# Both halves merged together: branch and output weights loaded once, the output projection by row tiles, the second norm's sums on ScalarE

## The chip, the cores and the metric

The kernel runs on one core of a Trainium2 chip. The metric is the device time of one execution in microseconds (us), here the median of three runs; 0.2% of it is 3.1 us. The engines are TensorE (PE: matmuls and transposes), VectorE (DVE), ScalarE (ACT), GpSimd (POOL) and SyncE (SP, which here only issues transfers). Each runs its own list of instructions in order; a row at the head of a list that waits holds up all behind it. Operands lie in SBUF (128 partitions), matmul results in PSUM.

## The reference, cut to what matters

```python
# S = D = 1024, one sequence, one layer
proj = h @ w_in                       # q, k, v of two attention branches, two gates
o_a  = forgetting_attention(...)      # (S, 512): rows 0..3 of o in tiles of 128
o_c  = chunk_band_attention(...)      # (S, 512): rows 4..7 of o
merged = sigmoid(gate_a) * (o_a @ w_br_fox) + sigmoid(gate_c) * (o_c @ w_br_chunk)
mix  = merged @ w_out
x    = layer_norm(alpha * x + (1 + g1) * mix, ln1_g, ln1_b)
h    = layer_norm(x) * (1 + sc2) + sh2
u    = causal_depthwise_conv(h @ w_up, conv_w, conv_b)
...                                   # silu(a) * val, @ w_down, third norm
```

The change concerns the lines from `merged` to `h`.

## The kernel before, in words

All matmuls are float32 products made of three passes: each operand is split into a high and a low part (`hi`, and `lo = x - hi`), and the product is hi·hi + lo·hi + hi·lo (`mm3`, L192 to L194, and three matmuls in `add`, L954 to L956). One matmul takes a 128x128 block against 512 columns. The sequence is worked on in two halves of 512 tokens. Tiles stand transposed (channels on partitions) up to the merge.

The stage runs between the last gate products (psg) and the main up-projection. For each half:

- `load_o` brings o in four pairs of tiles (4, 6, 2, 0; 4 to 7 belong to the second branch): raw o from DRAM (`ost`, 512 KB), the softmax factors r broadcast over rows (`ort`, two transfers of 256 KB), their product on VectorE (L793), the high part on ScalarE (`oh`, L796), the low part on VectorE (`ol`, L797).
- `merge` makes, for each of eight column tiles c, two branch products (psb; branch 1 then branch 0, four k tiles each, 12 matmuls a branch) from the branch weights `brd[c]` (two transfers of 512 KB, high and low), multiplies each with its gate (`sgl`, read from `gd`, L928), adds the two (L934) and splits the sum (`mh` on ScalarE L937, `ml` on VectorE L938).
- `mix` is the output projection: eight k tiles of weights `wod[k]` (two transfers each) against four row tiles, two column halves (psm). Half 0 goes through k on the outside and four row tiles inside; half 1 takes k = 0 so, and the other k row tile by row tile, with more buffers for the weights (`wide`). Then per row tile the residual (L981, L982).
- `norms` makes two layer norms per row tile: the first with gain and bias (L991, L992), stored to `xd`; the second without (`normalise`: sums by bn_stats L119, final scaling on ScalarE L140). For half 0 it is stepped inside merge(1), one step per c, so VectorE has it between the gate products.
- `turned_0` and `turned_1` transpose the second norm's result (L1004), scale it by the modulation (L1006) and split it into operands: half 0's `ha`, `hb` and half 1's differences `hc`.

Then come eight heads (`head`, psu, L859), each 24 matmuls, whose weights are split by `ready` (L847, L848); turned_1 is stepped between them, its first step ahead of all heads that follow the first two.

The order of each engine's list is set by the framework's scheduler from the order in which the program is written and from its own estimates; the buffers of a pool (`bufs`) decide when a transfer may be issued. All transfers of weights, gates, o and x in this stage are issued by SP, one list. Half 1's o is read during mix(0), one pair per k from the third on:

```python
reading = load_o(1, o1, (4, 6, 2, 0), mx, "xr", 4, mx, "xr")
xs0 = mix(0, m0, chain((None,) * 2, reading))
beside = norms(0, xs0, x0)
m1 = merge(1, o1, beside, ahead)
```

Of the kernel before, what the change touches and what calls it, by code (L numbers as in the profile page):

```python
# [19 lines left out]
P = 128  # L20
# [24 lines left out]
def body(ctx, tc, a, out):  # L45
# [735 lines left out]
    sy.dma_start(out=g1row, in_=rowd[0].partition_broadcast(P))  # L781
    o_cm, op_ = opened(name="o", bufs=1, side="right")

    def load_o(half, os_, pairs, pool, tag, bufs, rpool, rtag, early=0):
        for n, i in enumerate(pairs):
# [3 lines left out]
            rt = rpool.tile([P, 2, H], F32, name=nm("ort"), tag=rtag, bufs=4)  # L789
# [13 lines left out]
    reading = load_o(0, o0, (4, 6, 2, 0), ap0, "qs", 4, ap0, "m1", 3)  # L803
# [13 lines left out]
    h_11, h_21 = operands(hap, "ha"), operands(hap, "hb")  # L817
# [3 lines left out]
    mx_cm, mx = opened(name="mx", bufs=2)  # L821
# [46 lines left out]
    def ready(c, pool=None, raws_in=None):  # L868
# [8 lines left out]
        st = raws_in.tile([P, 2, H], F32, name=nm("sgl"), tag="sgl", bufs=2).rearrange("p j (k n) -> p (j k) n", k=4)  # L877
# [24 lines left out]
    if True:  # L902
# [11 lines left out]
        def merge(half, os_, beside, ahead=iter(())):  # L914
            ms = []
            held = {}

            def branch(c, b):
                if c not in held:
                    sg = mx.tile([P, 2, H], F32, name=nm("sgl"), tag="sgl", bufs=2)  # L920
                    sy.dma_start(out=sg, in_=gd[half, 2 * c : 2 * c + 2].rearrange("b p s -> p b s"))
                    held[c] = [x.rearrange("p j (k n) -> p (j k) n", k=4) for x in parted_w(brd[c])], sg
                (bh, bl), sg = held[c]
                ps = mxp.tile([P, H], F32, name=nm("psb"), tag="mm")
                for k in range(4):
                    kk = 4 * b + k
                    mm3(ps, bh[:, kk, :], bl[:, kk, :], os_[kk][0], os_[kk][1], k == 0, k == 3)
                ve.scalar_tensor_tensor(out=sg[:, b, :], in0=sg[:, b, :], scalar=1.0, in1=ps, op0=ALU.add, op1=ALU.mult)  # L928

            for c in range(KD):  # L930
                branch(c, 1)
                branch(c, 0)
                sg = held.pop(c)[1]
                ve.tensor_tensor(out=sg[:, 0, :], in0=sg[:, 0, :], in1=sg[:, 1, :], op=ALU.add)  # L934
                mh = mx.tile([P, H], F32R, name=nm("mh"), tag=f"mh{c}", bufs=1)
                ml = mx.tile([P, H], F32R, name=nm("ml"), tag=f"ml{c}", bufs=1)
                se.copy(out=mh, in_=sg[:, 0, :])  # L937
                ve.tensor_sub(out=ml, in0=sg[:, 0, :], in1=mh)  # L938
                ms.append((mh, ml))
                next(ahead, None)  # L940
                next(beside, None)
            return ms

        def mix(half, ms, beside, wide=None, ended=None, rest=None):
            ps = [
                [(mxt if t == 3 else mxp).tile([P, H], F32, name=nm("psm"), tag="tt" if t == 3 else "mm") for _ in range(2)]
                for t in range(4)
            ]

            def add(t, k, w):  # L950
                mh, ml = ms[k]
                ts = slice(t * P, (t + 1) * P)
                for n in range(2):
                    pe.matmul(ps[t][n], mh[:, ts], w[0][:, n, :], start=k == 0, stop=False)  # L954
                    pe.matmul(ps[t][n], mh[:, ts], w[1][:, n, :], start=False, stop=False)
                    pe.matmul(ps[t][n], ml[:, ts], w[0][:, n, :], start=False, stop=k == end)  # L956

            end = 3 if wide else KD - 1
            late = []
            for k in range(1 if wide else KD):  # L960
                w = parted_w(wod[k])
                for t in range(4):
                    add(t, k, w)
                next(beside, None)
            if wide:
                late += [(k, parted_w(wod[k])) for k in (1, 2)]
                late += sorted(wide.items()) + [(k, parted_w(wod[k], rest)) for k in (6, 7)]
# [6 lines left out]
            if wide:  # L974
                late.append((3, parted_w(wod[3])))
# [484 lines left out]
```

## Time and profile before

| | |
|---|---|
| timed, median of three | 1547.22 us (1544.13 to 1547.38) |
| span of the profiled execution | 1548.2 us |
| TensorE busy | 1502.7 us, 97% |
| VectorE / ScalarE busy | 1034.5 us, 67% / 709.5 us, 46% |
| chain that ended last | PE 72%, POOL 9%, DMA 8%, DVE 7% |
| transfers | 317.54 MB, mean 205 GB/s |

The profile is of one execution, its time 1.0 us over the median of the timed ones. Times on its axis are us from the start of the span. A matmul's record overlaps the next one's: 0.39 us is from start to end, and what counts in a row of matmuls is the distance of their starts. "Granted clock" (PEclk) is TensorE's clock as a share of 2.4 GHz; it has the two levels 1.00 and .50 (1.2 GHz), and a window that holds both shows a value between. A wait in the profile names what ended it. "Idle before" on an engine that nobody waits for costs nothing.

### The profile page before, as it was taken

The page shows a single profiled execution, that of the slowest core. Times are in us where ns is not written, and L with a number is a line of the kernel's source. Part 1 is how long each engine was busy: PE and PEld are TensorE (multiplying, and loading weights), DVE is VectorE, ACT ScalarE, POOL GpSimd, SP SyncE. Part 2 cuts the span into 40 slices and gives each one's busy share as a digit, 9 for nine tenths or more (in the row PEclk, how much of TensorE's full clock was granted, in tenths as well). Part 3 has the DMA queues.
Part 4 walks back from the last instruction along what each step waited for, and adds up shares of the span by engine and source line. Part 5 has one row for each costly group of instructions (what it writes and reads, how often), then busy time and mean ns, then how long its engine had stood idle before and what let it go on. Part 6 is the DMA issues. An engine that isn't in the chain of part 4 may idle for free.

```text
span 1548.2 us, 21760 instructions
## 1 busy us (share of the span) xinstructions
PE 1502.7 (97%) x7663; PEld 1264.7 (82%) x7663; DVE 1034.5 (67%) x2038; ACT 709.5 (46%) x1316; POOL 658.2 (43%) x607
## 2 busy tenths in 40 slices
PE   6999999999999999999998999999999999999996
PEld 3788898889889888888886877888888888888885
DVE  6756566566656565554468587777778776845798
ACT  3545555554544454442112165544544554555451
POOL 0039897787878776730000005454455443000000
PEclk9999999999999999999999999999999999999998
DMA  9156666756576578758999575443344322697552
GB/s 366 50 165 215 217 192 198 218 194 216 189 233 220 189 260 299 260 151 292 308 323 347 214 258 190 140 154 132 122 140 147 115 102 104 246 328 255 191 190 75
DMA packets 129756, 317.54 MB, mean 205 GB/s; under 512 B 13024, under 2 KB 21936, under 8 KB 129648
## 3 DMA queue, kind: packets, MB, share of 16 engines
q1 hardware_dynamic: 90208, 197.83, 37.8%
q0 software_dynamic: 25344, 92.02, 17.8%
q10 hardware_dynamic: 14096, 26.31, 4.8%
q8 instruction: 60, 0.98, 0.3%
q14 instruction: 48, 0.39, 0.1%
HBM read 223.47 MB, written 84.25 MB: 199 GB/s over the span
## 4 chain that ended last, share of the span: by engine, by line
PE 72%; POOL 9%; DMA 8%; DVE 7%; issue 2%; ACT 1%; SPq 0%; ACTq 0%; DVEq 0%; POOLq 0%
PE psu L859 25%; PE psd L1277 4%; PE psd L1278 4%; PE psd L1276 4%; PE pso L508 3%; DMA wod<-dr 3%; PE psg L192 3%; PE psg L194 3%; PE psg L193 3%; POOL dr L553 2%; PE pst L494 2%; POOL acc L559 2%; POOL dr L556 2%; PE psq L194 2%; DMA brd<-dr 2%
## 5 line engine op out<-in xcount | busy, mean ns | idle before, releaser
L859 PE MATMUL psu<-hc,wx 128*128 128x512 f32 x792 | 185.7, 389 | 0.1
L859 PEld LDWEIGHTS psu<-hc,wx 128*128 128x128 f32 x792 | 148.6, 188 | 31.3 <-ACT u L1202 0.5
L1125 DVE SCALAR_TENSOR_TENSOR pcv<-u,convp,pcv 128x1024 f32<-128x1024 f32 x88 | 113.1, 1286 | 45.4 <-ACT pcv L1123 44.4
L1266 DVE TENSOR_TENSOR op<-rw,op 128x512 fp32r<-128x512 f32 x146 | 93.4, 687 | 52.8 <-ACT op L1265 52.5
L1265 ACT CAST op<-rw 128x512 fp32r<-128x512 f32 x146 | 85.2, 622 | 85.4 <-PE psd L1278 39.8
L457 ACT ACTIVATE s<-s,mx 128x640 f32<-128x640 f32 (+7 forms) x128 | 94.5, 738 | 58.6 <-DVE mx L451 57.4
L1277 PE MATMUL psd<-op,op 128*128 128x512 f32 x292 | 113.6, 389 | 0.9 <-DVE op L1266 0.9
L1278 PE MATMUL psd<-op,op 128*128 128x512 f32 x292 | 113.6, 389 | 0.0
L1276 PE MATMUL psd<-op,op 128*128 128x512 f32 x292 | 113.1, 389 | 0.0
L497 ACT CAST pt<-pst 128x512 fp32r<-128x512 f32 (+1 forms) x192 | 82.1, 450 | 62.3 <-PE pst L494 60.8
L498 DVE TENSOR_TENSOR pt<-pst,pt 128x512 fp32r<-128x512 f32 (+1 forms) x192 | 96.0, 519 | 17.2 <-ACT pt L497 15.5
L192 PE MATMUL psq<-h1h,wh 128*128 128x512 f32 x256 | 103.8, 407 | 1.7 <-DVE h1h L188 1.3
L192 PE MATMUL psg<-h1h,wh 128*128 128x512 f32 x256 | 103.7, 405 | 0.0
L194 PE MATMUL psq<-h1h,wl 128*128 128x512 f32 x256 | 100.9, 394 | 0.9 <-DVE wl L112 0.9
L194 PE MATMUL psg<-h1h,wl 128*128 128x512 f32 x256 | 100.3, 392 | 0.5 <-DVE wl L112 0.5
L193 PE MATMUL psq<-h1l,wh 128*128 128x512 f32 x256 | 100.8, 394 | 0.0
L193 PE MATMUL psg<-h1l,wh 128*128 128x512 f32 x256 | 100.2, 391 | 0.0
L556 POOL TENSOR_SCALAR dr<-dr,cond 128x512 f32<-128x512 f32 x56 | 89.9, 1607 | 8.1 <-DMA dr<-in_w_ada 7.1
L508 PE MATMUL pso<-pt,vs 128*128 128x256 f32 x608 | 90.4, 288 | 1.3 <-DVE pt L498 1.2
L994 POOL DMA_DIRECT2D xd<-xr x8 | 4.4, 545 | 199.3 <-DVE xr L992 199.3
L508 PEld LDWEIGHTS pso<-pt,vs 128*128 128x128 f32 x608 | 81.1, 191 | 8.7 <-DVE pt L498 2.6
L112 DVE TENSOR_TENSOR wl<-ws,wh 128x1024 fp32r<-128x1024 f32 x38 | 61.2, 1611 | 39.1 <-ACT wh L111 39.1
(286 smaller groups left out, 4001.3 us busy)
## 6 DMA issues: line engine op xcount, KB each, us to landing
ws<-in_w_up SPq DMA_DIRECT2D x34, 512.0 KB, 3.7
dr<-in_w_ada POOLq DMA_DIRECT2D x32, 512.0 KB, 4.8
dr<-in_w_down POOLq DMA_DIRECT2D x22, 512.0 KB, 4.8
td<-dr POOLq DMA_DIRECT2D x22, 512.0 KB, 4.7
rw<-td SPq DMA_DIRECT2D x44, 256.0 KB, 4.5
yd<-y SPq DMA_DIRECT2D x20, 512.0 KB, 2.7
rw<-yd SPq DMA_DIRECT2D x40, 256.0 KB, 4.2
rw<-sd SPq DMA_DIRECT2D x33, 256.0 KB, 4.6
```

The costliest lines, as they stand in the source:

```text
L192: pe.matmul(ps, wh, xh, start=start, stop=False)
L193: pe.matmul(ps, wh, xl, start=False, stop=False)
L194: pe.matmul(ps, wl, xh, start=False, stop=stop)
L457: se.activation(out=st[:, 0:nk], in_=st[:, 0:nk], func=AF.Exp, scale=-1.0, bias=prev, accum_out=sums[:, col : col + 1])
L498: ve.tensor_sub(out=dl, in0=src, in1=dh)
L508: pe.matmul(ps[:, 0:256], vs[:, h % 2, j0 + j, :], pt[j // 4][:, c, j % 4, :], start=j == 0 and c == 0, stop=j == nj - 1 and c == 1)
L556: po.tensor_scalar_mul(x[:, k % 2, :] if k else acc, x[:, k % 2, :], cond[:, k : k + 1])
L859: pe.matmul(ps, w[:, a_, k, :], h[k][b_], start=first, stop=k == 3 and a_ == 1, skip_group_check=on)
L1125: ve.scalar_tensor_tensor(out=ps, in0=u[b][:, 2 - d : S + 2 - d], scalar=cp[:, 2 - d : 3 - d], in1=ps, op0=ALU.mult, op1=ALU.add)
L1276: pe.matmul(ps[t], g[:, 0, ts], d[:, 0], start=start, stop=False, skip_group_check=on)
L1277: pe.matmul(ps[t], g[:, 0, ts], d[:, 1], start=False, stop=False, skip_group_check=on)
L1278: pe.matmul(ps[t], g[:, 1, ts], d[:, 0], start=False, stop=stop, skip_group_check=on)
```

## The change

- Both halves are merged in one pass: for c = 0 and 1 all of half 0's units come first, then half 1's; for c from 2 on each c is done for half 0 and half 1. Half 1's o is read during the first four units, through two staging buffers that later hold output weights. Each `brd[c]` is loaded once.
- The merged tiles of both halves stay in SBUF, and so do all eight `wod[k]`, loaded once.
- The output projection goes by row tiles over the whole sequence: tiles 0 and 1 together, then 2 to 7 one at a time, each over all k. Residual and norms of a tile follow it.
- For tiles 0 to 6 the second norm's sum and sum of squares are made by ScalarE (Identity and Square with an accumulated output, L989 and L994 of the new kernel), its root by `rooted`; tile 7 keeps `normalise`.
- Half 0's transposes are stepped after the row tiles 5 and 6, through the transposes' own PSUM buffers; half 1's first step comes after the third head in place of before it.

```diff
-    def load_o(half, os_, pairs, pool, tag, bufs, rpool, rtag, early=0):
+    def load_o(half, os_, pairs, pool, tag, bufs, rpool, rtag, op_, early=0):
...
-            rt = rpool.tile([P, 2, H], F32, name=nm("ort"), tag=rtag, bufs=4)
+            rt = rpool.tile([P, 2, H], F32, name=nm("ort"), tag=rtag, bufs=bufs)
...
+            order_ = [(0, 1, 0), (0, 0, 0), (1, 1, 0), (1, 0, 0), (0, 1, 1), (1, 1, 1), (0, 0, 1), (1, 0, 1)]
+            order_ += [(c, b, half) for c in range(2, KD) for half in range(2) for b in (1, 0)]
+            for n, unit in enumerate(order_):
+                branch(*unit)
+                if n < 4:
+                    next(reading)
...
+        def norms(t, xx, x2, on_act):
...
+            se.activation(out=x2, in_=xx, func=AF.Identity, accum_out=s1)
+            yield
+            ve.tensor_scalar_mul(nmean, s1, -1.0 / D)
+            se.activation(out=x2, in_=xx, func=AF.Square, bias=nmean, accum_out=s2)
+            yield
+            ve.tensor_scalar(out=v, in0=s2, scalar1=1.0 / D, scalar2=EPS, op0=ALU.mult, op1=ALU.add)
+            r = rooted(v)
+            ve.tensor_tensor(out=b, in0=nmean, in1=r, op=ALU.mult)
+            se.activation(out=x2, in_=xx, func=AF.Identity, scale=r, bias=b)
...
-        m0 = merge(0, o0, iter(()))
-        reading = load_o(1, o1, (4, 6, 2, 0), mx, "xr", 4, mx, "xr")
-        xs0 = mix(0, m0, chain((None,) * 2, reading))
-        beside = norms(0, xs0, x0)
-        m1 = merge(1, o1, beside, ahead)
-        turning = turned_0(x0)
-        xs1 = mix(1, m1, iter(()), wide, turning, hdp)
+        ms = merge((o0, o1), load_o(1, o1, (4, 6, 2, 0), wop, "wh", 2, wop, "wl", o1p))
+        ws = [parted_w(wod[k], wop) for k in range(2)] + [parted_w(wod[k]) for k in range(2, 5)]
+        ws += [parted_w(wod[k], w2p) for k in range(5, KD)]
+        for group in ((0, 1), (2,), (3,), (4,), (5,), (6,), (7,)):
+            rows(min(NT, group[-1] + 3))
+            for k in range(KD):
+                for i, t in enumerate(group):
+                    mixed(t, ws, ms, ps[i], k)
+            if turning:
+                for _ in range(2):
+                    next(turning, None)
+            for i, t in enumerate(group):
+                residual(ps[i], xs[t])
+            for t in group:
+                begin(t)
+            if group == (4,):
+                turning = turned_0(x2s)
+            if group == (6,):
+                for c in range(EARLY):
+                    ready(c, hdp, mx)
...
-    next(turns)
     for c in range(EARLY, HEAD):
         head(c)
         next(turns, None)
```

TensorE at the start of the merge, before: from half 0's c = 1 (weights wh_7958) to its c = 2 (ws_7997, loaded ahead); oh and ol are tiles of half 0's o.

```order
L194 MATMUL psb_7976<-oh_7810,wl_7959 128x512
L192 MATMUL psb_8001<-oh_7790,ws_7997 128x512
L193 MATMUL psb_8001<-ol_7791,ws_7997 128x512
L194 MATMUL psb_8001<-oh_7790,ws_7998 128x512
...
L192 MATMUL psb_8001<-oh_7800,ws_7997 128x512
...
L192 MATMUL psb_8015<-oh_7876,ws_7997 128x512
L193 MATMUL psb_8015<-ol_7877,ws_7997 128x512
```

TensorE at the same place after the change: oh_7936 is half 1's pair 4, oh_7965 pair 6, oh_8024 pair 0, oh_7995 pair 2; ws_8098 is c = 2.

```order
L194 MATMUL psb_7999<-oh_7813,wl_7970 128x512
L192 MATMUL psb_8030<-oh_7936,wh_7910 128x512
L192 MATMUL psb_8046<-oh_7936,wh_7969 128x512
...
L192 MATMUL psb_8030<-oh_7965,wh_7910 128x512
L192 MATMUL psb_8046<-oh_7965,wh_7969 128x512
...
L192 MATMUL psb_8060<-oh_8024,wh_7910 128x512
L192 MATMUL psb_8079<-oh_8024,wh_7969 128x512
...
L192 MATMUL psb_8060<-oh_7995,wh_7910 128x512
...
L192 MATMUL psb_8104<-oh_7793,ws_8098 128x512
```

After 48 matmuls of half 0 come half 1's units of c = 0 and 1 in the order of pairs 4, 6, 0, 2; c = 2 of half 0, which followed at once before, stands behind all of them.

SP's list at the same place, before: wh_7958 and wl_7959 are the weights of c = 1, ost_8323 the first pair of half 1's o.

```order
L911 DMA wh_7958<-brd 128x2x512
L911 DMA wl_7959<-brd 128x2x512
L921 DMA sgl_7917<-gd 128x2x512
L921 DMA sgl_7956<-gd 128x2x512
L911 DMA wh_8036<-brd 128x2x512
L911 DMA wl_8037<-brd 128x2x512
L788 DMA ost_8323<-od 128x2x512
L921 DMA sgl_7995<-gd 128x2x512
```

SP's list after: the four pairs of half 1 are ost_7930, ost_7959, ost_7989 and ost_8018; sgl are gates.

```order
L913 DMA wl_7970<-brd 128x2x512
L926 DMA sgl_7914<-gd 128x2x512
L789 DMA ost_7930<-od 128x2x512
L793 DMA ort_7932<-rd 64x2x512 x2
L789 DMA ost_7959<-od 128x2x512
L793 DMA ort_7961<-rd 64x2x512 x2
L926 DMA sgl_7973<-gd 128x2x512
L789 DMA ost_7989<-od 128x2x512
...
L789 DMA ost_8018<-od 128x2x512
...
L926 DMA sgl_8044<-gd 128x2x512
```

Behind c = 1's weights the o loads of half 1 have moved up, ahead of the gates and weights of the later c; the third and fourth pair use the staging buffers of the first and second.

VectorE at that place after the change: L794 is the product with r, L798 the low part of o, L932 the gate product, L935 and L941 sum and split of a merged tile.

```order
L794 TENSOR_TENSOR ost_7930<-ost_7930,ort_7932 128x1024
L798 TENSOR_TENSOR ol_7937<-ost_7930,oh_7936 128x1024
L794 TENSOR_TENSOR ost_7959<-ost_7959,ort_7961 128x1024
L932 SCALAR_TENSOR_TENSOR sgl_7973<-sgl_7973,psb_7975 128x512
L932 SCALAR_TENSOR_TENSOR sgl_7973<-sgl_7973,psb_7999 128x512
L798 TENSOR_TENSOR ol_7966<-ost_7959,oh_7965 128x1024
L935 TENSOR_TENSOR sgl_7973<-sgl_7973 128x512
L941 TENSOR_TENSOR m_8015<-sgl_7973,m_8014 128x512
L794 TENSOR_TENSOR ost_7989<-ost_7989,ort_7991 128x1024
...
L794 TENSOR_TENSOR ost_8018<-ost_8018,ort_8020 128x1024
```

Before, no work on half 1's o stood here:

```order
L797 TENSOR_TENSOR ol_7877<-ost_7870,oh_7876 128x1024
L928 SCALAR_TENSOR_TENSOR sgl_7917<-sgl_7917,psb_7923 128x512
L928 SCALAR_TENSOR_TENSOR sgl_7917<-sgl_7917,psb_7937 128x512
L934 TENSOR_TENSOR sgl_7917<-sgl_7917 128x512
L928 SCALAR_TENSOR_TENSOR sgl_7956<-sgl_7956,psb_7962 128x512
L938 TENSOR_TENSOR ml_7953<-sgl_7917,mh_7952 128x512
L928 SCALAR_TENSOR_TENSOR sgl_7956<-sgl_7956,psb_7976 128x512
...
L928 SCALAR_TENSOR_TENSOR sgl_7995<-sgl_7995,psb_8001 128x512
```

The low part of the second pair (ol_7966) now stands behind two gate products (sgl_7973), and the fourth pair's product behind that.

VectorE in the second merge before: L119, L121, L123 and L127 to L139 are half 0's second norm; L928, L934 and L938 are the merge.

```order
L938 TENSOR_TENSOR ml_8859<-sgl_8823,mh_8858 128x512
...
L119 BN_STATS st_8867<-xr_8505 128x6
...
L928 SCALAR_TENSOR_TENSOR sgl_8886<-sgl_8886,psb_8892 128x512
L121 BN_AGGR mv_8870<-st_8867 128x2
L119 BN_STATS st_8930<-xr_8507 128x6
...
L928 SCALAR_TENSOR_TENSOR sgl_8886<-sgl_8886,psb_8906 128x512
...
L119 BN_STATS st_8930<-xr_8507 128x6
...
L934 TENSOR_TENSOR sgl_8886<-sgl_8886 128x512
...
L119 BN_STATS st_8989<-xr_8509 128x6
...
L938 TENSOR_TENSOR ml_8922<-sgl_8886,mh_8921 128x512
```

VectorE in the last c of the merge after the change:

```order
L932 SCALAR_TENSOR_TENSOR sgl_8472<-sgl_8472,psb_8474 128x512
L932 SCALAR_TENSOR_TENSOR sgl_8472<-sgl_8472,psb_8488 128x512
L935 TENSOR_TENSOR sgl_8472<-sgl_8472 128x512
L941 TENSOR_TENSOR m_8504<-sgl_8472,m_8503 128x512
L932 SCALAR_TENSOR_TENSOR sgl_8507<-sgl_8507,psb_8509 128x512
L932 SCALAR_TENSOR_TENSOR sgl_8507<-sgl_8507,psb_8523 128x512
L935 TENSOR_TENSOR sgl_8507<-sgl_8507 128x512
L941 TENSOR_TENSOR m_8539<-sgl_8507,m_8538 128x512
```

No row of a norm stands between the gate products any more.

## Rows read from the trace of the kernel before

**Rows 1.** Page, part 1: engine, busy us, share of span, instructions.
```profile
PE 1502.7 (97%) x7663; PEld 1264.7 (82%) x7663; DVE 1034.5 (67%) x2038; ACT 709.5 (46%) x1316; POOL 658.2 (43%) x607
```

**Rows 2.** Windows of 20 us: busy time per engine, PEclk, DMA share, GB/s.
```profile
820.00:840.00 20.00, 14.83 (x64) 11.33 (x62) 18.05 (x45) 3.94 (x8) 1.07 (x2) 0.98 0.99 370
...
920.00:940.00 20.00, 17.05 (x74) 13.24 (x73) 19.72 (x33) 16.84 (x30) 0.00 (x0) 0.91 0.48 169
```

**Rows 3.** TensorE's waits, 680 to 960 us: total, times, longest.
```profile
PE psb L192 <- DVE st L119: 2.5, 1, 2.5
PE psu L859 <- DVE wh L848: 2.1, 2, 1.6
PE psb L194 <- DMA wl<-brd: 1.7, 1, 1.7
PE psb L194 <- DMA ws<-brd: 1.4, 1, 1.4
```

**Rows 4.** Timeline, TensorE: start, us, line, tiles, count, idle before.
```profile
707.67 0.39 PE L192 MATMUL psb<-oh,wh 128*128 128x512 f32 x1
...
794.71 0.39 PE L192 MATMUL psb<-oh,wh 128*128 128x512 f32 x1
...
893.89 1.91 PE L1004 MATMUL pst<-ident,x 128*128 128x128 f32 x16
895.55 1.62 PE L859 MATMUL psu<-ha,hw 128*128 128x512 f32 x6
...
907.05 2.88 PE L859 MATMUL psu<-ha,wh 128*128 128x512 f32 x12
909.77 2.65 PE L859 MATMUL psu<-hb,wl 128*128 128x512 f32 x11
...
949.73 1.52 PE L859 MATMUL psu<-hc,wx 128*128 128x512 f32 x6
```

**Rows 5.** Windows of 2 us, columns as in rows 2.
```profile
838.00:840.00 2.00, 1.01 (x4) 0.49 (x4) 2.00 (x8) 0.04 (x1) 0.00 (x0) 0.79 0.78 287
840.00:842.00 2.00, 1.57 (x4) 1.29 (x5) 2.00 (x8) 1.36 (x3) 0.28 (x1) 0.50 0.93 324
842.00:844.00 2.00, 2.00 (x6) 1.52 (x5) 1.14 (x9) 2.00 (x3) 0.26 (x1) 0.50 1.05 406
844.00:846.00 2.00, 2.00 (x6) 1.60 (x5) 0.87 (x3) 0.07 (x1) 0.00 (x0) 0.50 1.07 410
846.00:848.00 2.00, 2.00 (x10) 1.64 (x10) 0.33 (x3) 1.25 (x1) 0.00 (x0) 1.00 0.35 131
```

**Rows 6.** Timeline of SP's DMA queue.
```profile
707.64 0.36 SPq L911 DMA_DIRECT2D wh<-brd  x1
...
708.56 0.97 SPq L921 DMA_DIRECT2D sgl<-gd  x2
```

**Rows 7.** Timeline of ScalarE and its queue.
```profile
708.50 0.38 ACTq L386 DMA_DIRECT2D gd<-sg  x1
```

**Rows 8.** Tile ort (r's rows), 700 to 960 us, issue to landing.
```profile
DMA to landing us min/median/max: 5.9/6.2/8.1
```

**Rows 9.** Tile sgl (gates), 700 to 850 us, issue to landing.
```profile
DMA to landing us min/median/max: 3.6/5.6/10.6
```

**Rows 10.** Groups by line and form, 700 to 960 us.
```profile
L928 DVE SCALAR_TENSOR_TENSOR sgl<-sgl,psb 128x512 f32<-128x512 f32 x32 | 21.6, 682 | 25.9 <-DMA sgl<-gd 13.6 <-PE psb L194 12.2
...
L140 ACT ACTIVATE x<-xr,nb,r 128x1024 f32<-128x1024 f32 x8 | 9.8, 1242 | 4.9 <-DVE nb L139 4.9
L797 DVE TENSOR_TENSOR ol<-ost,oh 128x1024 fp32r<-128x1024 f32 x8 | 9.6, 1224 | 6.8 <-ACT oh L796 6.8
...
L796 ACT CAST oh<-ost 128x1024 fp32r<-128x1024 f32 x8 | 8.2, 1049 | 26.5 <-DVE ost L793 24.8 <-issue 1.7
...
L793 DVE TENSOR_TENSOR ost<-ost,ort 128x1024 f32<-128x1024 f32 x4 | 4.9, 1225 | 15.6 <-DMA ort<-rd 15.6
```

**Rows 11.** Timeline of VectorE in the heads.
```profile
936.46 1.89 DVE L1016 TENSOR_TENSOR hc<-ht,hc 128x512 fp32r<-128x512 f32 x3
```

More of the change, by code (lines that the diff above doesn't have):

```diff
@@ L937, in merge @@
                 se.copy(out=mh, in_=sg[:, 0, :])
                 ve.tensor_sub(out=ml, in0=sg[:, 0, :], in1=mh)
-                ms.append((mh, ml))
-                next(ahead, None)
-                next(beside, None)
-            return ms
[L944 to L967, printed above, removed]
-            xs = []
-            for t in range(4):
-                tt = 4 * half + t
-                xx = mx.tile([P, D], F32, name=nm("xr"), tag="xr", bufs=4)
-                sy.dma_start(out=xx, in_=a["x"][tt * P : (tt + 1) * P, :])
-                xs.append(xx)
-            if wide:
-                late.append((3, parted_w(wod[3])))
-            for t in range(4):
-                for k, w in late:
-                    add(t, k, w)
-                for n in range(2):
-                    ns = halves(n)
-                    ve.tensor_tensor(out=ps[t][n], in0=ps[t][n], in1=g1row[:, ns], op=ALU.mult)
-                    ve.scalar_tensor_tensor(out=xs[t][:, ns], in0=xs[t][:, ns], scalar=ALPHA, in1=ps[t][n],
-                                            op0=ALU.mult, op1=ALU.add)
-                if t and ended is not None:
-                    next(ended, None)
-            return xs
@@ L1060, in body @@
[L1060 to L1071 removed]
+        sy.dma_start(out=l1g, in_=a["ln1_g"].partition_broadcast(P))
+        sy.dma_start(out=l1b, in_=a["ln1_b"].partition_broadcast(P))
@@ new lines, in body, with begin @@
+        rows(4)
+        live = []
+        def begin(t):
+            x2s.append((mx if t < 4 else mxb).tile([P, D], F32, name=nm("x2"), tag="x2", bufs=4))
+            for g in live:
+                next(g, None)
+            g = norms(t, xs[t], x2s[t], t < NT - 1)
+            next(g)
+            for old in live:
+                next(old, None)
+            live[:] = [g]
+        turning = None
+        for group in ((0, 1), (2,), (3,), (4,), (5,), (6,), (7,)):
+            rows(min(NT, group[-1] + 3))
+            ps = [[mxp.tile([P, H], F32, name=nm("psm"), tag="mm") for _ in range(2)] for _ in group]
+            for k in range(KD):
[9 more added lines that the diff above has]
+            if group == (4,):
+                h_11 += operands(hap, "ha")
+                h_21 += operands(hap, "hb")
+                turning = turned_0(x2s)
+            if group == (6,):
+                for c in range(EARLY):
+                    ready(c, hdp, mx)
```

135 lines of the change are left out of this document (82 added, 53 removed).

## The prediction

> **What bounds the kernel now.** I read the page first: TensorE is busy for 97% of the span [rows 1], so a change can win only where the matmuls stand still, and loses where it makes them stand still. Then the windows by 20 us, to find the stage of the change and how full each engine is in it: the reader is to see TensorE below 20 us in two windows, and VectorE near full in the same two [rows 2]. Then TensorE's waits over the stage, each with its releaser [rows 3]: two weight transfers (wl and ws from brd), one sum of the norms (st, L119) and, at the end, weight splits (wh, L848). Last the timeline of TensorE, which gives the borders [rows 4].
>
> The stage runs from 707.67 (first branch product) to 949.73 (first main product), 242.1 us. Its work: 384 branch, 384 output and 192 head matmuls, and 64 transposes. Twelve matmuls start in 2.72 us (907.05 to 909.77), so one is 0.2267 us; sixteen transposes take 1.66 us, so one is 0.104 [rows 4]. Part by part:
> - merge and mix of half 0, 707.67 to 794.71: 87.04 us for 384 x 0.2267 = 87.05. Nothing is lost, so one loading of the weights instead of two wins nothing here.
> - merge and mix of half 1, 794.71 to 893.89: 99.18 us for 87.05 + 1.7 (16 transposes). Lost 10.4.
> - heads, 893.89 to 949.73: 55.84 us for 192 x 0.2267 + 48 x 0.104 = 48.5. Lost 7.3.
>
> In all 17.7 us. About 1.6 of it is spread in tenths (changes between transposes and matmuls).
>
> **Where the change can win.** In half 1's merge VectorE works on half 0's norms between the gate products, and weights come late: 2.5 + 1.7 + 1.4 us of waits [rows 3], and the granted clock falls to .50 (1.2 GHz) from about 839 to 846, after TensorE was busy for only 1.01 of 2 us; it was busy 1.57 to 2.00 in the windows at .50 [rows 5], and half of those 5.6 us is 2.8 lost. The change takes out all of this: no norm lies in the merge any more (the VectorE rows of the order), and brd and wod pass once, 32 transfers of 512 KB fewer. I put the middle after it at 1.4: 0.9 of tenths that stay, and 0.5 for transposes of half 0 that wait for the third tile. TensorE needs 48 x 0.2267 = 10.9 us per row tile. VectorE has six rows of 512 at 0.60 [rows 11], two of 1024 at about 1.2 [rows 10] and some fifteen narrow ones per tile, 8 to 9 us, and stays under it; bounds 0.9 to 4.
>
> **Where it pays: the start of the merge.** Before, TensorE went from half 0's c = 0, 1 to c = 2, whose operands lay ready, and half 1's o was loaded under mix(0), with 40 us to spare. Now half 1's o is wanted after 48 matmuls, at 707.67 + 10.88 = 718.55, and its transfers are issued only behind the brd pair that SP can issue at 707.64 and the gates at 708.56 [rows 6], as the SP rows of the order show. TensorE has nothing else in front: c = 2 stands behind all four loads. Step by step (A, B, C, D are pairs 4, 6, 2, 0; the staging has two buffers):
> - A: ost at about 709.0, the two ort at 709.5 and 710.1. An ort took 5.9, 6.2 or 8.1 from issue to landing [rows 8]; I take 8.1 with five transfers in front: 718.2. Times r (1.225, L793), cast to oh (1.049, L796): 720.5. TensorE waits 2.
> - B: its second ort stands behind a wait for the last gate tile's store, which ScalarE issues at 708.50 [rows 7]; with 5.6, the median of the gates' transfers [rows 9], 714.5. Landed +8.1 = 722.6, oh at 724.9. Its difference ol is queued on VectorE behind two gate products whose gates are issued after it (715.1, landed about 723.7): 2 x 0.682, then 1.224 (L928, L797 [rows 10]): 726.3.
> - D has to wait for B's buffer: last ort issued at 727.4, +6.2 (the queue is empty now) = 733.6, oh at 735.9. C used A's buffer and is there earlier, but TensorE's order wants D first.
> - Then 24 matmuls, 5.4, and 0.8 of waiting for ol: 742.1, against 707.67 + 96 x 0.2267 = 729.4 without waits.
>
> That is 12.7 lost; with the landings spaced as they drain in the queue I get 11.9. I take 12. Bounds: with 3.6, the shortest gate transfer, for both landings, D's oh is there at 728.6 and 5.4 are lost; with 10.6 for B and 8.1 for D, 17 [rows 8, 9].
>
> To this comes the clock. TensorE stands some 2, 1, 1 and 7 us; the last is longer than any wait of before. The fall after the pair of waits at 835 to 839 cost 2.8 [rows 5], and a shorter stretch of half clock is seen in the heads (.91 in 920 to 940 [rows 2]: 0.09 x 20 = 1.8). I take 2.3; bounds 0 to 6.
>
> One rule speaks against this order. The rows first: across the 1.7-us wait for wl the clock stayed at 1.00 (820 to 840 has .98 [rows 2], and the 0.02 x 20 us it lacks are those from 838 to 840), and it fell only after two waits close together [rows 3, 5]. The Trainium skill, "TensorE: Matmul & The Clock Gate", section "HAM oscillation — how this bites in real kernels", says that where short runs of matmuls alternate with waits for transfers, the clock can fall at each wait and each run starts slow. The rows bear that out only for the longer waits.
>
> **The tail.** After the last output matmul TensorE has 192 head matmuls and 32 transposes, 46.9 us. VectorE has in its order 54 rows of 512 for heads, turns and weights. Three in a row take 1.89, the last of them 0.68, so they start 0.60 apart [rows 11]: 32.4. Residual and norm of tile 7 (eight rows of 512 at 0.60, two of 1024 at 1.2, and narrow ones that wait for each other) I put at 12, the weight sum and tile 6's rest at 2 to 4: 46 to 49. So VectorE is as late as it was before (19.72 of 20 us in 920 to 940 [rows 2]). ScalarE gets two more passes of 1.24 per tile [rows 10] in place of VectorE's two sums of tiles 0 to 6, but tile 7 keeps the old way, and this one sets the tail. The first turn comes one head later, which gives tile 7 time. I take 6.0 for 7.3; bounds 3 (only tenths and one wait) and 11.
>
> **Sum.** 12 + 2.3 + 1.4 + 6.0 = 21.7 lost, against 17.7: +4.0 on the profiled 1548.2, that is 1552.2. The median of the timed runs (1547.22) is 1.0 below the span, so 1551.2. TensorE's order has 6719 rows in both, and I cost the rest at nothing: the x rows, l1g and l1b come under the merge, which has 16 MB less to load.
>
> **Rivals.** Faster or slower means over 0.2% (3.1 us), about what three runs can tell from no change.
> - The second half's o comes early. Place: D's oh; the transfers meet an emptier queue since brd's c = 2 is already in. Landings of 3.6 us lose 5.4, all waits are short and the clock stays: 5.4 + 0 + 1.4 + 6.0 = 12.8, 4.9 under before: 1542.3, faster. For it: the shortest transfers [rows 9]. Against: eight ort never took under 5.9 [rows 8]. It decides from a start that costs under 10.3.
> - Gain and loss cancel. Landings of 4.9, halfway between 3.6 and 6.2: 8.0 + 2.3 + 1.4 + 6.0 = 17.7: 1547.2, no change. For it: a transfer with few others is shorter than the median, and B and D each count once.
> - The tail gets worse: ScalarE's passes for tile 6 (Identity, Square and the scaling, with narrow VectorE rows between them) stand before the first heads' copies and tile 7's scaling: four passes of 1.24 more, 5: 1556.2. For it: ScalarE was the releaser in the tail only little [rows 3], so there is no room known; against: it is free when the tail starts.
> - The clock falls at each wait of the start, by the mechanism of the rule above: at A, B and D, 2.3 each, 4.6 more: 1555.8. For it: three waits within 18 us; against: the 1.7-us wait that left the clock alone.
>
> **Chances.** Forecast 0.33, early o 0.24, cancelling 0.28, worse tail 0.09, clock at each wait 0.06. Faster 0.24, same 0.28, slower 0.48. The forecast's own range is 1549 to 1555. The range to hold 8 in 10 reaches from just under the early case to over the two dear ones: 1541 to 1559.
>
> **What would show it.** TensorE's waits near 718 to 736 on oh (L797 of the new kernel, ScalarE's cast) and ol, one of 5 us or more, with the brd and wod loads no longer among its releasers, and VectorE's L119 gone from them. The clock at .50 for some us near 735. TensorE without idle from c = 2 to the last output row tile, apart from tenths. The first main product 4 us later than 949.73. I am wrong if D's oh is there before 731, if wod or the norms hold TensorE in the row tiles (a wait of over 1 us on psm), or if the heads wait over 8 us.

## The result, and the profile after

The changed kernel took 1553.51 us (median of 20 runs, 1550.13 to 1558.57), the kernel before 1548.57 in the same session (20 runs, 1543.85 to 1555.16). The ratio is 1.0032 with an interval of 1.002 to 1.0043: 5.0 us slower (3.1 to 6.7), where +4.0 was forecast.

The two profiled spans hide this: 1548.6 us after against 1548.2. The execution profiled after happened to reach the stage earlier, at 703.96 against 707.67 [rows 4], with the same code in front; over all traces of this study that moment lies between 703.96 and 713.74. So traces are compared from the first branch product on. To the first main product it is 242.06 us before and 243.85 after, from there to the first psd matmul (the last projection, with `w_down`; L1308 of the new kernel) 375.73 and 378.01: 617.79 and 621.86 in all, +4.07.

TensorE's busy time hardly moved [rows 1]; ScalarE has 16 us more, VectorE 3 less:

```profile
PE 1500.3 (97%) x7663; PEld 1264.7 (82%) x7663; DVE 1031.5 (67%) x2024; ACT 725.5 (47%) x1344; POOL 658.6 (43%) x607
```

TensorE's waits from 680 to 960 us (total, times, longest), which answer to [rows 3]:

```profile
PE psb L192 <- ACT oh L797: 10.7, 2, 7.4
PE psu L861 <- ACT wx L849: 2.0, 1, 2.0
PE psu L861 <- DVE u L1189: 1.5, 1, 1.5
PE psb L193 <- DVE ol L798: 0.9, 2, 0.5
```

The waits for brd and for the norms are gone, those for half 1's o have come, and nothing in the heads waits; the first main product does. TensorE's timeline gives the new borders, as in [rows 4] (start, duration, count, and in brackets the idle time before the row and its releaser):

```profile
703.96 0.39 PE L192 MATMUL psb<-oh,wh 128*128 128x512 f32 x1
...
718.33 0.77 PE L192 MATMUL psb<-oh,wh 128*128 128x512 f32 x2 [3.33 <-ACT oh L797]
...
734.20 1.22 PE L192 MATMUL psb<-oh,wh 128*128 128x512 f32 x2 [7.38 <-ACT oh L797]
...
742.37 0.39 PE L192 MATMUL psb<-oh,ws 128*128 128x512 f32 x1
...
898.52 2.88 PE L861 MATMUL psu<-ha,hw 128*128 128x512 f32 x12
...
947.81 1.02 PE L861 MATMUL psu<-hc,wx 128*128 128x512 f32 x3 [2.03 <-ACT wx L849]
...
958.62 2.88 PE L861 MATMUL psu<-ha,wl 128*128 128x512 f32 x12
```

- Start (to c = 2): 96 matmuls from 703.96 to 742.37, 38.4 us for 21.8. Lost 16.6: 11.6 of waits, and 5.0 that the waits don't hold.
- Middle: 742.37 to 898.52, 156.15 for 155.7. Lost 0.5.
- Heads: 898.52 to 947.81, 49.3 for 46.9. Lost 2.4, of which 2.0 is the wait for wx that ends them.
- The first 36 main matmuls: 10.81 us (947.81 to 958.62); before they took 8.16. Lost 2.65, of which 2.28 is left at the first psd.

The 5.0 of the start is nearly all the clock. Windows of 2 us, columns as in [rows 5]:

```profile
718.00:720.00 2.00, 1.17 (x3) 0.70 (x4) 1.23 (x1) 0.28 (x1) 0.00 (x0) 0.72 1.05 246
720.00:722.00 2.00, 2.00 (x6) 1.52 (x6) 1.38 (x2) 0.12 (x1) 0.00 (x0) 0.50 0.74 232
...
728.00:730.00 2.00, 0.00 (x0) 0.00 (x0) 1.23 (x1) 0.62 (x1) 0.00 (x0) 0.78 1.06 206
...
732.00:734.00 2.00, 0.00 (x0) 0.00 (x0) 1.67 (x2) 0.89 (x1) 0.00 (x0) 0.50 1.06 393
...
736.00:738.00 2.00, 2.00 (x6) 1.55 (x5) 0.01 (x1) 0.00 (x0) 0.00 (x0) 0.50 1.00 364
```

It falls to 1.2 GHz twice, behind the wait of 3.33 us and inside that of 7.38; in 720 to 722 and 736 to 738 TensorE is busy throughout, and by its timeline a matmul starts every 0.43 us instead of every 0.2267. Behind the first wait, 9 matmuls take 3.7 us without their waits, 1.7 too much; from 734.20 to 742.37, 24 take 8.17, 2.7 too much. Only the second loss moves the end of the start: the first lies ahead of the wait for pair D, and D's oh came 30.2 us after the stage began, however fast TensorE was before it (e11 shows it). In windows of 20 us the stage's middle, and the heads that stood at .91 [rows 2], are now full:

```profile
740.00:760.00 20.00, 20.00 (x90) 16.57 (x89) 11.10 (x17) 2.49 (x4) 0.00 (x0) 1.00 0.89 298
...
920.00:940.00 20.00, 20.00 (x102) 16.80 (x102) 19.69 (x33) 16.34 (x28) 0.00 (x0) 1.00 0.61 208
```

SP's queue shows why half 1's o is late, beside [rows 6]: pairs A and B go out at once behind c = 1's weights and a gate, C at 719.57 and D at 724.22, when buffers come free:

```profile
703.93 0.36 SPq L913 DMA_DIRECT2D wh<-brd  x1
...
708.26 2.82 SPq L793 DMA_DIRECT2D ort<-rd  x2
...
719.57 0.36 SPq L789 DMA_DIRECT2D ost<-od  x1
...
724.22 0.37 SPq L789 DMA_DIRECT2D ost<-od  x1
```

Tile ort, 690 to 760 us, issue to landing; against [rows 8] the slowest grew. B's second one took 10.0:

```profile
DMA to landing us min/median/max: 4.7/6.4/10.9
```

### The profile page after: what moved, and what is told of

Read it like the earlier page. It is cut to its first block, busy times and chain, and to the rows that moved or that the text cites. A ratio compares the mean times of both kernels' runs of the same rounds, so it can differ in the third digit from the quotient of the medians.

```text
span 1548.6 us, 21684 instructions
## 1 busy us (share of the span) xinstructions
PE 1500.3 (97%) x7663; PEld 1264.7 (82%) x7663; DVE 1031.5 (67%) x2024; ACT 725.5 (47%) x1344; POOL 658.6 (43%) x607
## 4 chain that ended last, share of the span: by engine, by line
PE 74%; POOL 9%; DMA 8%; DVE 5%; issue 2%; ACT 1%; SPq 0%; DVEq 0%; ACTq 0%; POOLq 0%
PE psu L861 24%; PE psd L1309 4%; PE psd L1310 4%; PE psd L1308 4%; PE pso L508 3%; PE psg L192 3%; PE psg L194 3%; PE psg L193 3%; DMA wod<-dr 3%; POOL dr L553 2%; PE pst L494 2%; POOL acc L559 2%; POOL dr L556 2%; DMA brd<-dr 2%; PE psm L957 2%
## 5 line engine op out<-in xcount | busy, mean ns | idle before, releaser
L1308 PE MATMUL psd<-op,op 128*128 128x512 f32 x292 | 113.1, 389 | 0.0
L494 PE MATMUL pst<-ident,s 128*128 128x128 f32 x528 | 83.1, 273 | 0.8 <-DVE pt L498 0.7
```

Source lines behind the costliest of these rows:

```text
L494: pe.transpose(ps[:, b * P : (b + 1) * P], st[:, c0 : c0 + P], ident)
L1308: pe.matmul(ps[t], g[:, 0, ts], d[:, 0], start=start, stop=False, skip_group_check=on)
```

## The experiments

"Stage" is the time from the first branch product to the first psd, in the one execution that was profiled; the ratio is that of the timed runs to the kernel before, timed beside them. The two differ by up to 2.8 us (e9: -3.1 in the trace, about -5.9 timed), so a difference of 1 or 2 us of stage is not clear by itself.

| | stage us | against 617.79 | ratio | interval |
|---|---|---|---|---|
| changed kernel | 621.86 | +4.1 | 1.0032 | 1.0020 to 1.0043 |
| e1_early_o | 620.16 | +2.4 | 1.0028 | 1.0010 to 1.0045 |
| e2_three_c | 613.17 | -4.6 | 0.9981 | 0.9965 to 0.9997 |
| e3_sums_dve | 621.96 | +4.2 | 1.0039 | 1.0021 to 1.0057 |
| e4_before_sums_act | 616.42 | -1.4 | 0.9998 | 0.9984 to 1.0012 |
| e5_early_pool | 616.30 | -1.5 | 1.0001 | 0.9988 to 1.0013 |
| e6_early_pool_start | 619.41 | +1.6 | 1.0026 | 1.0012 to 1.0040 |
| e7_twice | 642.22 | +24.4 | 1.0155 | 1.0139 to 1.0172 |
| e8_turn_back | 620.45 | +2.7 | 1.0019 | 1.0005 to 1.0032 |
| e9_early_c2_back | 614.65 | -3.1 | 0.9962 | 0.9946 to 0.9977 |
| e10_three_c_back | 612.12 | -5.7 | 0.9961 | 0.9943 to 0.9978 |
| e11_filled | 619.03 | +1.2 | 1.0015 | 0.9996 to 1.0034 |
| e12_ready_first | 614.49 | -3.3 | 0.9979 | 0.9965 to 0.9992 |

**e1_early_o**: all four pairs of half 1's o are fetched ahead of the merge, by SP, into the room of the merged tiles.

```diff
+    fetched = [
+        fetch_o(1, i, *[m1p.tile([P, 2, H], F32, name=nm(g), tag=f"m{2 * n + q}") for q, g in enumerate(("ost", "ort"))], sy)
+        for n, i in enumerate((4, 6, 2, 0))
+    ]
...
```

> The changed kernel with one thing moved: half 1's o and its factors r are fetched while the last gate tiles are still multiplied, right behind half 0's last pair, into the room where half 1's merged tiles will lie; products and splits stay where they were. Theory (the loss sits at the start of the merge, 16 us of waits and half clock there): TensorE no longer waits for oh or ol, the clock stays at 1.00 until the main product, 14 to 17 us under the changed kernel, about 1537 to 1539, so faster than the kernel before by 9 to 12 us. Rival 1 (the 4 MB only change places in the queues: brd of c = 1 and the gates land late instead): TensorE waits 5 to 10 us for wh, wl or sgl near the first 24 matmuls, 1543 to 1549. Rival 2 (the loss sits in the heads and at the start of the main product): 1552 or more.

No wait for oh is left, and one for c = 1's weights is there in its place. TensorE's wait, SP's issue of those weights, and windows of 10 us:

```profile
PE psb L192 <- DMA wh<-brd: 13.2, 1, 13.2
```

```profile
713.77 0.36 SPq L924 DMA_DIRECT2D wh<-brd  x1
```

```profile
700.00:710.00 10.00, 10.00 (x46) 8.27 (x45) 3.75 (x4) 2.94 (x4) 0.00 (x0) 1.00 1.06 277
710.00:720.00 10.00, 0.60 (x3) 0.17 (x1) 5.33 (x5) 2.09 (x2) 0.00 (x0) 0.68 1.06 265
```

The weights stand behind the o loads in SP's queue while the DMA engines are full, at only 265 to 277 GB/s. The longest wait has moved and grown. The first rival held in kind, but the wait and the time were above its ranges.

**e2_three_c**: c = 2 of half 0 goes ahead of half 1's units, so 72 matmuls lie in front instead of 48.

```diff
-            order_ = [(0, 1, 0), (0, 0, 0), (1, 1, 0), (1, 0, 0), (0, 1, 1), (1, 1, 1), (0, 0, 1), (1, 0, 1)]
-            order_ += [(c, b, half) for c in range(2, KD) for half in range(2) for b in (1, 0)]
+            order_ = [(c, b, 0) for c in range(3) for b in (1, 0)] + [(c, 1, 1) for c in range(3)]
+            order_ += [(c, 0, 1) for c in range(3)]
+            order_ += [(c, b, half) for c in range(3, KD) for half in range(2) for b in (1, 0)]
```

> The changed kernel with 72 matmuls of half 0 (c = 0, 1, 2) ahead of half 1's c = 0, 1, 2, in place of 48 ahead of c = 0, 1; transfers as they were. Theory (half 1's o arrives some 30 us after the stage begins, whatever TensorE does, and the cost is what TensorE lacks to fill that time): 24 matmuls more are 5.4 us of cover, the first wait (3.3) goes, the long one falls from 7.4 to about 5, half clock of one fall is saved; but the weights of c = 3 wait for c = 0's buffers and may cost 1 to 3. 4 to 8 us under the changed kernel, about 1546 to 1550. Rival (the queue is what is late, and the gates of c = 2 put o back by as much): 1552 to 1555.

```profile
PE psb L192 <- ACT oh L797: 5.4, 2, 4.9
```

The wait halves, and the stage is 8.7 us shorter than in the changed kernel: the start is where the change pays, and the order of the units sets how much. Timed, e2 is also faster than the kernel before (its interval ends at 0.9997).

**e3_sums_dve**: the changed kernel with every norm's sums on VectorE again.

```diff
-            g = norms(t, xs[t], x2s[t], t < NT - 1)
+            g = norms(t, xs[t], x2s[t], False)
```

> The changed kernel with the second norm's sums of all tiles on VectorE again (one part undone). Theory (VectorE has some 8 to 9 us of work per row tile of 10.9 us on TensorE, 2.5 more with the sums, so it is at the limit): TensorE waits in the row tiles or at the first transposes, 0 to 5 us in all, 1553 to 1558. Rival 1 (ScalarE's passes were what made the changed kernel slower): 1549 or less. Rival 2 (VectorE falls behind by the sums of all tiles, and the heads pay for it): 1560 or more.

The stage differs by 0.1 us and the ratio by less than its interval; its longest wait of TensorE:

```profile
PE psb L192 <- ACT oh L797: 10.8, 2, 7.7
```

The sums on ScalarE neither win nor cost anything that can be measured here, where they stand behind the merge.

**e4_before_sums_act**: the kernel before with the sums of half 0's second norm on ScalarE, and nothing else; the first norm stays on VectorE between the gate products.

```diff
-                normalise(x2, xx, True)
+                s1 = small.tile([P, 1], F32, name=nm("s1"), tag="mx", bufs=8)
+                se.activation(out=x2, in_=xx, func=AF.Identity, accum_out=s1)
...
+                se.activation(out=x2, in_=xx, func=AF.Square, bias=nmean, accum_out=s2)
...
```

> The kernel before with only half 0's second norm sums moved to ScalarE (one part done alone). Theory (in the second merge TensorE waited because VectorE had the sums between the gate products): the 2.5 us wait on st and the fall of the clock after it (2.8) go, the waits for wl and ws of brd (3.3) stay: 3 to 5 us under the kernel before, 1543 to 1546. Rival (the weights' waits take up what the sums leave): within 1.5 us of the kernel before.

The wait that the trace of before put down to the norm's sum (2.5 us, [rows 3]) stays, under another name:

```profile
PE psb L192 <- DVE ml L938: 2.6, 1, 2.6
PE psb L194 <- DMA wl<-brd: 2.1, 1, 2.1
```

The timelines of SP and TensorE, and the time from issue to landing of the first ws transfer (weights of c = 7; tile brd in a window around its issue), show what it really waited for. The kernel before, with VectorE's split ml ahead:

```profile
829.03 0.69 DVE L938 TENSOR_TENSOR ml<-sgl,mh 128x512 fp32r<-128x512 f32 x1
829.74 0.36 SPq L921 DMA_DIRECT2D sgl<-gd  x1
830.20 0.42 SPq L911 DMA_DIRECT2D ws<-brd  x1
DMA to landing us min/median/max: 7.5/7.5/7.5
837.85 0.47 PE L192 MATMUL psb<-oh,ws 128*128 128x512 f32 x1 [2.50 <-DVE st L119]
```

The same rows in e4:

```profile
827.64 0.36 SPq L921 DMA_DIRECT2D sgl<-gd  x1
828.10 1.27 SPq L911 DMA_DIRECT2D ws<-brd  x2
DMA to landing us min/median/max: 8.1/8.1/8.1
836.38 0.76 PE L192 MATMUL psb<-oh,ws 128*128 128x512 f32 x1 [2.56 <-DVE ml L938]
```

The weights came late. They landed at 837.7 and 836.2, and TensorE went on 0.15 and 0.2 us later; the rows of VectorE that the waits name only ended in the same moment. So the prediction's reading of this wait was wrong, and e4's rival (the weights) held. VectorE was not without a part: the weights stand in SP's list behind a gate, the gate's transfer needs one of two buffers, and in the kernel before it went out when VectorE had done the split ml (829.72). What VectorE does between the gate products can put weights back by this way; the first norm's rows, which e4 leaves there, were not tested. Up to the first head e4 is 1.8 us shorter than the kernel before (186.04 for 187.88), where the theory had 3 to 5 in all.

**e5_early_pool**: e1 with GpSimd issuing the fetches, so that no o stands ahead of brd in SP's queue; the diff is against e1.

```diff
-        fetch_o(1, i, *[m1p.tile([P, 2, H], F32, name=nm(g), tag=f"m{2 * n + q}") for q, g in enumerate(("ost", "ort"))], sy)
+        fetch_o(1, i, *[m1p.tile([P, 2, H], F32, name=nm(g), tag=f"m{2 * n + q}") for q, g in enumerate(("ost", "ort"))], po)
```

> e1_early_o with the early fetch of half 1's o issued by GpSimd in place of SP. In e1 the o loads stood in SP's list ahead of brd of c = 1, which then came 13.4 us late, and the DMA engines were full (share 1.06) at only 265 GB/s, some 4.8 us per pair. Theory (what was lost is the time of four pairs in a list that also holds the weights; GpSimd is idle there, so o comes early and brd of c = 1 is issued at once when the gates' weights are done with): no wait over 2 us in the first 96 branch matmuls, clock at 1.00, 13 to 17 us under the changed kernel: 1537 to 1541. Rival (the transfers are bound by the DMA engines, not by the list: brd and the gates land late behind 4 MB of o): waits of 4 to 9 us for wh, wl or sgl, 1543 to 1548.

TensorE's waits, and GpSimd's first fetch:

```profile
PE psb L192 <- DMA wh<-brd: 4.9, 1, 4.9
PE psb L194 <- DMA wl<-brd: 3.7, 1, 3.7
```

```profile
693.73 0.75 POOL L786 DMA_DIRECT2D ost<-od  x1 [13.38 <-PE pso L508]
```

SP issues brd at 703.98 and 704.45, without delay, yet the two land at 714.50 and 719.42: 10.5 and 15 us, against 4.3 and 5.2 in the changed kernel. The room comes free only when attention ends, so the fetches still fall into the merge, and there the engines are shared. The stage is 5.6 us better than in the changed kernel, but most of the expected gain (13 to 17) is gone to the same engines.

**e6_early_pool_start**: e5, whose diff is above, with the main product's first weights asked for ahead of the heads.

```diff
+    start = summed(order[0], slice(0, 4, 3), hbp, "fs"), raw(order[1], 1, hbp, "fs")
...
-        if c == EARLY:
-            start = summed(order[0], slice(0, 4, 3), hbp, "fs"), raw(order[1], 1, hbp, "fs")
```

> e5_early_pool with the first weights of the main product asked for ahead of the third head, as in the kernel before, and the turn left behind it. Theory (the 2.0, 0.4 and 1.5 us that the changed kernel waits at the start of the main product come from these operands being made after the last turn): 2 to 4 us under e5_early_pool. Rival (VectorE and ScalarE are full in the heads, so it only changes which work is late): within 1.5 us of e5_early_pool.

```profile
PE psu L872 <- ACT wx L860: 2.6, 1, 2.6
```

Against e5 the wait for wx grew from 1.9 to 2.6 and the stage by 3.1 us, which none of the expectations had. Asking earlier without the turn ahead of the third head does not help; why it costs 3 us stayed open.

**e7_twice**: the changed kernel with 14.7 MB of extra reads on GpSimd's queue during the middle, to see whether the 16 MB that the change saves were worth time.

```diff
+            for j in range(4 if paced else 0):
+                again = mxb.tile([P, H], F32, name=nm("again"), tag="h32", bufs=4)
+                po.tensor_copy(out=again[:, 0:1], in_=paced[0][:, 0:1].bitcast(F32))
+                po.dma_start(out=again, in_=src[j])
...
+                if half and c == 1:
+                    paced.append(ml)
```

> The changed kernel with 14.7 MB of extra reads: brd of c = 2 to 7 and all of wod are read a second time into tiles that nobody reads, issued by GpSimd after c = 1 of half 1 is merged. It puts back the traffic that the change takes away, and no wait of the computation. Theory (loading once gains nothing by itself; it is the order that costs and gains): within 2 us of the changed kernel, 1552 to 1555. Rival (the traffic was what made weights late in the second merge): waits for wl, ws or sgl of 2 us and more come back, 1557 or more.

A window of 20 us, then TensorE's longest wait, then VectorE's wait from 830 to 860 us:

```profile
800.00:820.00 20.00, 19.88 (x88) 16.16 (x87) 5.55 (x9) 1.24 (x2) 8.89 (x25) 1.00 1.02 378
```

```profile
PE psm L963 <- DVE xr L971: 12.6, 1, 12.6
```

```profile
DVE hw L883 <- ACT hw L882: 38.5, 2, 33.0
```

The time missed what was expected, but not through the traffic: from 740 to 820, at a DMA share of .92 to 1.04 in its four windows, TensorE was busy for 79.88 of 80 us. The extra reads stood in GpSimd's queue ahead of the first heads' weights, issued at 838 and 846 instead of 808 and 817; VectorE had those weights' split ahead of the residuals in its order and stood. So the run says that later weights (well ahead of their use) are not late at full engines; it says nothing clean on the saved 16 MB.

**e8_turn_back**: the changed kernel with the first turn, and the main product's first weights, ahead of the third head again.

```diff
+    next(turns)
+    start = summed(order[0], slice(0, 4, 3), hbp, "fs"), raw(order[1], 1, hbp, "fs")
...
-        if c == EARLY:
-            start = summed(order[0], slice(0, 4, 3), hbp, "fs"), raw(order[1], 1, hbp, "fs")
```

> The changed kernel with half 1's first turn and the first main weights ahead of the third head again (one part undone). Theory (the heads have room now, the second norm of tile 7 being the last thing needed): the transposes wait 0 to 3 us for tile 7, the main product starts 2 to 4 us earlier, so within 2 us of the changed kernel, 1551 to 1555. Rival 1 (the turn's move is what keeps TensorE from waiting in the heads): 1556 or more. Rival 2 (the move only costs): 1550 or less.

```profile
PE psu L861 <- DVE wh L850: 1.2, 1, 1.2
```

The waits of the main product are gone: from it to the first psd 375.36 us instead of 378.01. The heads wait again, and the way to the first main product is 1.2 longer, 0.8 of it at the start of the merge, which this run leaves alone. Net it is 1.4 us better in the trace, within the theory's total, but the main product did not start earlier as the theory had it. The timed intervals of the two kernels overlap.

**e9_early_c2_back**: e5 and e8 together, whose diffs are above, with half 0's c = 2 second in the order.

```diff
+            order_ = [(0, 1, 0), (0, 0, 0), (2, 1, 0), (2, 0, 0), (0, 1, 1), (2, 1, 1), (1, 1, 0), (1, 0, 0)]
+            order_ += [(1, 1, 1), (0, 0, 1), (2, 0, 1), (1, 0, 1)]
```

> e5_early_pool with half 0's c = 2 (whose weights lie ready) and c = 0, 2 of half 1's pairs 4 and 6 ahead of c = 1, and with half 1's first turn where it was before (as in e8_turn_back). In e5 the o loads came early enough but brd of c = 1 landed 10.5 and 15 us after its issue, beside them. Theory (the four pairs and brd of c = 1 are some 5 MB that the DMA engines need until about 16 us after the stage begins, so the order must put 72 matmuls on operands that are there): no wait over 1.5 us until the heads, clock at 1.00, the first main product some 10 us earlier than in e5_early_pool after the stage's begin (228 to 231 in place of 238), 1536 to 1541. Rival (the gates and c = 3 are late in turn): waits of 4 us and more in the first 20 us or at c = 3, 1544 to 1549.

```profile
PE psb L194 <- DMA wl<-brd: 4.3, 1, 4.3
PE psb L192 <- DMA wh<-brd: 4.0, 1, 4.0
```

Buffers are given in the order of the calls, so c = 2 now got the pair that is loaded late, and the wait of e5 stayed. Timed it is among the best all the same (6 us under before); the trace gives 3.1.

**e10_three_c_back**: e2 and e8 together; its edits are theirs.

> e2_three_c with half 1's first turn and the first main weights ahead of the third head, as in the kernel before. e2 lost 9 us in all, 3 of them at the start of the main product; e8 took those away and lost 1.8 in the heads. Theory (both act alone): 0 to 2 us under e2_three_c, 1542 to 1546. Rival (in e2 the heads come with less slack for tile 7 and wait more): 1547 or more.

```profile
PE psb L192 <- ACT oh L797: 6.1, 1, 6.1
PE psu L861 <- DVE wh L850: 1.2, 1, 1.2
```

The gains add up (9.7 us of stage below the changed kernel; 8.7 and 1.4 alone). At 0.9961 it beats both kernels, level with e9 in time, and it has the shortest stage of all.

**e11_filled**: the changed kernel with 14 and 28 idle matmuls in front of the units that wait, to hold the clock.

```diff
+                if n in (4, 6):
+                    idle = mxt.tile([P, H], F32, name=nm("idle"), tag="tt")
+                    for i in range((0, 14, 28)[n // 2 - 1]):
+                        pe.matmul(idle, held[1][0][:, 4, :], o0[4][0], start=True, stop=True)
```

> The changed kernel with 42 idle matmuls on operands that are there, into a PSUM tile that nobody reads: 14 ahead of half 1's first product, 28 about the second pair and ahead of the fourth. They take away no wait; they only keep TensorE busy in it. Theory (4 to 5 of the 16 us lost at the start are half clock after the two long waits): the clock stays at 1.00 in most of the stretch, the products after the waits start 0.23 apart, 2 to 4 us under the changed kernel, 1549 to 1551. Rival (the matmuls after the waits are held by ol and the gates, not by the clock): 1552 to 1556, the same or slower.

Windows of 10 us:

```profile
720.00:730.00 10.00, 10.00 (x45) 8.26 (x46) 7.31 (x8) 2.72 (x3) 0.00 (x0) 1.00 0.85 234
730.00:740.00 10.00, 7.49 (x33) 5.91 (x32) 5.11 (x6) 1.16 (x2) 0.00 (x0) 1.00 0.80 281
```

TensorE's product behind the wait for D:

```profile
734.26 0.73 PE L192 MATMUL psb<-oh,wh 128*128 128x512 f32 x2 [2.52 <-ACT oh L797]
```

The clock stays at 1.00 throughout, and the way to the main product is 2.8 us shorter. D's product starts 30.15 us after the stage began (704.11), against 30.24 in the changed kernel: the operands are as late as before, and the 2.8 is what the second fall of the clock cost (2.7 by its matmuls). The first fall cost nothing in the end, since the wait for D took it up. The rest of the loss is the operands' lateness, which no clock gives back. The timed intervals of the two kernels overlap (1.0015 and 1.0032).

**e12_ready_first**: e9 with c = 2 on the pair that lies loaded, and half 0's first gates on ScalarE's queue.

```diff
+                    on = se if not half and c in (0, 2) else sy
+                    on.dma_start(out=sg, in_=gd[half, 2 * c : 2 * c + 2].rearrange("b p s -> p b s"))
...
+            hold(0)
+            gate(0, 0)
+            gate(2, 0)
+            hold(1)
+            hold(2)
...
```

> e9_early_c2_back with the buffers given out so that the order does what it was meant to: in e9 the buffers followed the order of the calls, so that c = 2 got the pair that waits for the gates' weights and the pair loaded ahead lay ready for c = 1, unused for 15 us. Now c = 0, 1, 2 ask for their weights in that order and c = 2, loaded ahead, is multiplied second; the gates of half 0's c = 0 and 2 are issued by ScalarE, beside SP's brd of c = 1. Theory (with operands that lie ready for 72 matmuls, some 16 us, no transfer is late): waits under 3 us in the first 30 us and the clock at 1.00, the first main product 229 to 232 us after the first branch product (239 in e9), 1535 to 1541. Rival (the gates, 17 us from issue to landing in e9, hold the PSUM tiles): a wait of 3 to 6 us for a gate product near 721, 1541 to 1545.

TensorE's wait; VectorE's wait from 700 to 740 us; tile sgl, 690 to 745 us:

```profile
PE psb L193 <- DVE ol L805: 8.4, 1, 8.4
```

```profile
DVE sgl L956 <- DMA sgl<-gd: 10.3, 1, 10.3
```

```profile
DMA to landing us min/median/max: 3.6/15.0/20.1
```

Now the gates are late: VectorE waits for one with ol queued behind it. The rival held, with a longer wait than it had: in every order tried with the early fetch, some operand other than oh came late.

## Why the prediction was right

- **Start.** Forecast: 12 of late operands and 2.3 of clock, 14.3; measured 16.6. A's oh was there 14.3 us after the stage began (forecast 12.8), D's 30.2 (28.2), and the waits came on oh and ol where they were named. From D's oh on, the loss parts into 13.9 of lateness and 2.7 of clock, as the forecast reckoned it. So the term mis-sized is D's arrival: B's second ort was issued 6.5 us after the stage began (forecast 6.8) but took 10.0 us to land instead of 8.1, and D waited for B's buffer. The clock was nearly right in size. It fell a second time, behind the 3.33-us wait, which is the mechanism of the fourth rival at two of its three places (the third wait, 0.4 us at 724, left the clock at 1.00); but that fall was taken up by the wait for D, and not paid for (e11).
- **Why the start costs what it does.** In e1 the engines moved 5.4 MB in the 20 us from 700 to 720 at a share of 1.06 (277 and 265 GB/s, 10 us each). Half 1's o is 4.2 MB (four pairs of 512 KB of o and as much of r), and c = 1's weights and two gates are 2.1 more: an estimated 23 us of full engines, against 48 matmuls in front (10.9 us), of which 24 need c = 1's weights themselves. In the changed kernel the two staging buffers add to it: D's load could go out only at 724.22, and from 724 to 726 the engines were at .64. Before, the o came under mix(0). Fetching it earlier or from another queue mostly named another operand (oh 10.7 us; brd 13.2, then 4.9 + 3.7; ol 8.4), while e2's 24 more matmuls in front took 8.7 us off.
- **Middle.** Forecast 1.4 lost, measured 0.5: nearly all of half 1's 10.4 is won, and no wait on psm is among TensorE's. But the reason given for part of it, TensorE waiting for the norm's sum, was wrong (e4): the weights were late, behind a gate in SP's list, at a DMA share of .99 [rows 2]. What cleared them stays open. The merged form has no norms between the gate products, half the loads, and also four gate buffers in place of two (L925), which the prediction does not name; no run takes these apart. e7 speaks against the loads, since with 14.7 MB put back TensorE stood still for 0.12 us from 740 to 820.
- **Tail.** Forecast 6.0 lost in the heads; measured 2.4 there and 2.65 in the main product behind them. The size nearly held, the place did not, and the sign "first main product 4 us later" failed with it: it came 1.8 later. With the first turn one head later, what came late was the main product's operands (wx, u), not the heads'; the prediction put nothing there. e8 put the turn back: the main product's waits went and the heads' came back, 1.4 net in the trace. That ScalarE's added passes would delay the tail (third rival) is ruled out by e3, where the tail is as long without them.
- **Sum.** 16.6 + 0.5 + 2.4 + 2.65 = 22.15 lost, against the forecast's 21.7 and before's 17.7. The forecast's +4.0 stands beside +4.07 in the traces, 5.0 (3.1 to 6.7) in the times. That they lie so close is luck: the start had 2.3 too little (1.9 of lateness, 0.4 of clock), and the middle (0.9) and the tail (0.95) too much; 0.4 of what was lost is made up before the first psd. The mechanism of the start, which decides the sign, is what was right.

## What to carry to other kernels

Work that is merged to load weights once wins only where loading held somebody up; ask first what the old split was hiding. Here it hid 4 MB of o under an output projection, and the merged form put them at a place where weights and gates were wanted too. With the transfer engines full at the stage's beginning, another issue order or queue moved the wait to another operand; what helped most was more work in front that needed none of them. And the releaser that a wait names is only the row that ended last: look at when the waiting row's transfers landed, and what held up their issue, before blaming an engine's work.

## What the runs showed of the hardware

- Full DMA engines did not mean one rate. With the broadcasts of r on the way, a share of 1.05 to 1.06 moved 206 to 277 GB/s (728 to 730 and 718 to 720 after, 700 to 720 in e1); with weights and gates alone, 364 to 393 at 1.00 to 1.06 (732 to 734 and 736 to 738 after). No run has the broadcasts by themselves, so that they are the cause is not shown.
- Transfers of different issuers slowed each other: with the fetches on GpSimd, c = 1's weights on SP took 10.5 and 15 us to land, for 4.3 and 5.2 in the changed kernel; spread over three queues, gates took up to 20.1. The Trainium skill, "DMA: Bandwidth & Descriptors", section "Issuing engines are not separate DMA queues", says that transfers run on the same 16 engines whoever starts them; e5 and e12 agree.
- The clock fell behind a single wait of 3.33 us and stayed through waits of 0.4 here and of 1.7 before [rows 3]; 42 idle matmuls in the waits kept it at 1.00 (e11). Waits of 2.5 to 2.6 us did both: the clock was .51 in the 2 us behind one in e4 (836 to 838) and 1.00 behind one in e11 (734 to 736).
